# Moving the normalized rows' tiles to the weights' address modulo 512 bytes

## The chip, the cores and the metric

The kernel runs on one core of one Trainium2 chip. The metric is the device time of one execution in microseconds. Before the change it is 1011.47 us, the median of three runs that lie between 1011.24 and 1011.87 us.

## What is computed

Two layers of a decoder trunk on 256 rows of 1024 float32 values. Each layer has three sub-layers, and each of them normalizes the rows, scales and shifts them by a conditioning vector, and adds a gated result back:

```
h = modulate(rms_norm(x, norm_ffn1[l]), sh1, sc1)
x = x + 0.5 * g1 * swiglu(h, ffn1_w_in[l], ffn1_w_out[l])      # 1024 -> 2 x 2816 -> 1024
h = modulate(rms_norm(x, norm_mix[l]), sh2, sc2)
x = x + g2 * token_mix(h, ..., mix_w_in[l], ..., mix_w_out[l])  # gMLP half and sparse attention half
h = modulate(rms_norm(x, norm_ffn2[l]), sh3, sc3)
x = x + 0.5 * g3 * swiglu(h, ffn2_w_in[l], ffn2_w_out[l])
...
return rms_norm(x, final_norm)
```

The nine vectors `sh`, `sc`, `g` of a layer are `silu(c) @ ada_w[l] + ada_b[l]`.

## The kernel before, in words

**Precision.** Every float32 product of rows and weights is made of three products in the type float32r: high part by high part, and the two mixed ones. A weight tile `raw` (128 partitions x 4096 bytes) comes in by a DMA, ScalarE writes its high part `whi` (L474), VectorE the rest `wlo` (L479). There are 7 raw buffers and 10 of each part. The rows after normalization and modulation lie transposed in `hThi` and `hTlo`, 8192 bytes a partition each: two batches of 128 rows, eight blocks of 128 features, 512 bytes a block. The gated activations of the feed-forward lie in `aThi` and `aTlo` in blocks of 512 bytes, too.

**Six phases, three kinds of matmul.** The phases are feed-forward, mixing, feed-forward in layer 0, and the same in layer 1.

- In a feed-forward's input projection (`joint_chunk`, L694) the weights are the stationary operand, in 128-column slices, and the rows move: 256 columns, made of 128 columns of each batch 4096 bytes apart. Each matmul has a weight load of its own. There are 3648 of them: 1056 in the first feed-forward and 864 in each of the others, 24 for a weight tile.
- In the other input projections (the first 512 columns of feed-forwards 2 to 4 in `ffn_gen`, the mixing's in `mix_gen`) and in the mixing's output projection the rows `hThi`, `hTlo` are stationary, and the weights move, 512 columns at a time (L515 to L517, helper `mm3`): 960 matmuls, 288 of them in `ffn_gen`, and 96 with 324 columns.
- In a feed-forward's output projection (`project`) `aThi`, `aTlo` are stationary and the weights move by the same three lines: 990 matmuls of 512 columns. In the last phase the second batch's second half is cut in two, and there 132 of these matmuls have 256 columns.

**Order.** The schedule is written out by hand: each engine works in the order of the program. Between weight tiles the conditioning weights `ada_w` are streamed through the same raw buffers, and VectorE sums them up in `aacc` (L459). SyncE issues nearly all DMAs.

**Addresses.** The pool `const` hands out its tiles one behind the other in the order of the code. In the built program `hThi` begins at byte 36544 of each partition and `hTlo` at 44736: both are 192 modulo 512. `x` and `xm` are 64 modulo 512, `ident` 128, `ones` 192. The tiles `raw`, `whi`, `wlo`, `aacc`, `vec`, `aThi`, `aTlo` lie in other pools behind it, and all begin at 0 modulo 512.

The lines of the matmuls in question:

```
T.matmul(o, wk[stat][col], mov[:, :, k, :], start=..., stop=False, ...)   # L694
T.matmul(ps, ahi, whi, start=first, stop=False)                            # L515
T.matmul(ps, ahi, wlo, start=False, stop=False)                            # L516
T.matmul(ps, alo, whi, start=False, stop=last)                             # L517
```

In each the first operand behind the output is the stationary one. In the names of a row, `bank<-hThi,whi`, the moving one stands first.

Of the kernel before, what the change touches and what calls it, by code (L numbers as in the profile page):

```python
# [9 lines left out]
F32 = mybir.dt.float32  # L10
# [6 lines left out]
P = 128  # L17
D = 1024
KD = D // P
DFF = 2816  # L20
KF = DFF // P
DEPTH = 2
# [77 lines left out]
def trunk(ctx, tc, x_in, c_in, pos_in, ada_w, ada_b, norm_ffn1, ffn1_w_in, ffn1_w_out,  # L100
# [3 lines left out]
    V, S, G, T = nc.vector, nc.scalar, nc.gpsimd, nc.tensor  # L104
    ctx.enter_context(tc.manual_schedule())
    const = ctx.enter_context(tc.tile_pool(name="const", bufs=1))
# [25 lines left out]
    V.memset(negm, 1.0)  # L132
    ones = const.tile([P, P], F32R, name="ones")
    V.tensor_copy(ones, negm[:, :P])
    mhalf = const.tile([P, 16], F32, name="mhalf")[:, :1]
    G.memset(mhalf, -0.5)

    def causal_mask():
        G.memset(negm, 0.0)
# [61 lines left out]

    x = [const.tile([P, D], F32, name=f"x{b}") for b in range(2)]
    xm = [const.tile([P, D], F32, name=f"xm{b}") for b in range(2)]
    cols = const.tile([P, DEPTH, 96], F32, name="cols")
    ab = const.tile([P, DEPTH, 3, 2, KD], F32, name="ab")
    accs = [None]
    hThi = const.tile([P, 2, KD, P], F32R, name="hThi")
    hTlo = const.tile([P, 2, KD, P], F32R, name="hTlo")
    ang = const.tile([P, 2, 8], F32, name="ang")
    hT = [(hThi[:, b], hTlo[:, b]) for b in range(2)]  # L210

# [1122 lines left out]
```

## Time and profile before

| | |
|---|---|
| median of the runs | 1011.47 us |
| the profiled execution's own time | 1015.82 us |
| its span | 1014.1 us |
| TensorE (PE) busy | 986.3 us, 97% |
| weight loads (PEld) busy | 881.0 us, 87% |
| VectorE (DVE) busy | 777.9 us, 77% |
| ScalarE (ACT) busy | 536.3 us, 53% |
| bytes moved by DMA | 253.41 MB, 250 GB/s |

The span is what the profile's rows cover; the profiled execution took 1.7 us more than that, and 4.35 us more than the median. Times in the rows count from the span's start. The busy time of PE counts matmuls by ends that are modelled and that overlap. How fast a dense stream of matmuls runs is therefore read from the distance between their starts, or from how many lie in a window, and not from the duration of one.

### The profile page before, as it was taken

The numbers are of one execution on the slowest core, as the hardware profiler recorded it, in microseconds if no ns is written. First come the engines' busy times: TensorE is split into PE (matmuls) and PEld (weight loads), VectorE is DVE, ScalarE is ACT, GpSimd is POOL, SyncE is SP. The second block draws the span as 40 slices with busy tenths as digits, with TensorE's granted clock in tenths as the row PEclk, the third lists the DMA queues.
The fourth block names the chain that finished last, engine by engine and source line by source line (L and its number), as shares of the span: only waits on it lengthen the run. The fifth ranks groups of instructions, "written<-read, shape, count | busy, mean of one in ns | idle before, by whom it ended". The sixth has DMA issues, their size and how long they took to land.

```text
span 1014.1 us, 16715 instructions
## 1 busy us (share of the span) xinstructions
PE 986.3 (97%) x6468; PEld 881.0 (87%) x6468; DVE 777.9 (77%) x1088; ACT 536.3 (53%) x804; POOL 26.4 (3%) x39
## 2 busy tenths in 40 slices
PE   7999997999999999999999999999999999999997
PEld 6899995887787899998888999878778889999886
DVE  6888988777897877789678688895878785576554
ACT  6465454356577744545455454543657765454341
POOL 4000000000000000000000000000000000000000
PEclk9999998999999999999999999989999999999999
DMA  9988899956655577889858779987554556576731
GB/s 333 380 286 321 316 352 353 356 181 225 188 189 157 169 270 280 300 314 356 289 162 315 276 291 344 358 328 235 167 152 138 166 158 207 169 252 243 262 115 42
DMA packets 110031, 253.41 MB, mean 250 GB/s; under 512 B 8754, under 2 KB 27236, under 8 KB 109952
## 3 DMA queue, kind: packets, MB, share of 16 engines
q1 hardware_dynamic: 109120, 251.20, 70.8%
q8 instruction: 50, 0.82, 0.3%
q0 software_dynamic: 544, 0.63, 0.3%
q10 hardware_dynamic: 288, 0.52, 0.1%
q14 instruction: 29, 0.24, 0.1%
HBM read 251.27 MB, written 1.05 MB: 249 GB/s over the span
## 4 chain that ended last, share of the span: by engine, by line
PE 73%; DVE 12%; DMA 7%; ACT 5%; issue 3%; POOL 0%; SPq 0%; POOLq 0%; ACTq 0%; DVEq 0%
PE bank L694 28%; PE bank L515 14%; PE bank L517 13%; PE bank L516 13%; DVE wlo L479 3%; DVE aacc L459 3%; PE bank L780 2%; DMA raw<-in_ffn_w_in_dram 2%; DMA raw<-in_ffn_w_out_dram 2%; DMA sraw<-in_ada_w_dram 2%; ACT whi L474 2%; DVE xm L717 1%; ACT aThi L511 1%; DMA raw<-in_ada_w_dram 1%; DVE aacc L1101 1%
## 5 line engine op out<-in xcount | busy, mean ns | idle before, releaser
L474 ACT ACTIVATE whi<-raw 128x1024 fp32r<-128x1024 f32 (+1 forms) x328 | 334.9, 1046 | 233.1 <-PE bank L517 126.6
L479 DVE TENSOR_TENSOR wlo<-raw,whi 128x1024 fp32r<-128x1024 f32 (+1 forms) x313 | 373.9, 1212 | 91.7 <-ACT whi L474 89.7
L694 PE MATMUL bank<-hThi,whi 128*128 128x256 f32 x1216 | 336.1, 280 | 1.6 <-ACT hThi L1139 1.6
L694 PE MATMUL bank<-hThi,wlo 128*128 128x256 f32 x1216 | 333.2, 277 | 0.0
L694 PE MATMUL bank<-hTlo,whi 128*128 128x256 f32 x1216 | 323.7, 277 | 0.0
L694 PEld LDWEIGHTS bank<-hThi,whi 128*128 128x128 f32 x1216 | 228.3, 188 | 2.9 <-ACT hThi L1139 2.0
L694 PEld LDWEIGHTS bank<-hThi,wlo 128*128 128x128 f32 x1216 | 229.1, 188 | 0.7 <-issue 0.7
L694 PEld LDWEIGHTS bank<-hTlo,whi 128*128 128x128 f32 x1216 | 222.6, 188 | 0.3
L515 PE MATMUL bank<-whi,aThi 128*128 128x512 f32 (+1 forms) x374 | 144.1, 385 | 1.4 <-ACT whi L474 1.3
L516 PE MATMUL bank<-wlo,aThi 128*128 128x512 f32 (+1 forms) x374 | 143.2, 383 | 2.3 <-DVE wlo L479 2.3
L459 DVE SCALAR_TENSOR_TENSOR aacc<-raw,ccol,aacc 128x1024 f32<-128x1024 f32 x112 | 143.5, 1281 | 1.2 <-DMA raw<-in_ada_w_dram 1.2
L517 PE MATMUL bank<-whi,aTlo 128*128 128x512 f32 (+1 forms) x374 | 142.7, 381 | 0.0
L515 PE MATMUL bank<-whi,hThi 128*128 128x512 f32 (+1 forms) x352 | 140.9, 400 | 0.7 <-ACT hThi L560 0.7
L517 PE MATMUL bank<-whi,hTlo 128*128 128x512 f32 (+1 forms) x352 | 136.2, 387 | 0.0
L516 PE MATMUL bank<-wlo,hThi 128*128 128x512 f32 (+1 forms) x352 | 135.1, 384 | 0.0
L516 PEld LDWEIGHTS bank<-wlo,aThi 128*128 128x128 f32 x374 | 71.4, 191 | 16.1 <-DVE wlo L479 3.3
L515 PEld LDWEIGHTS bank<-whi,aThi 128*128 128x128 f32 x374 | 71.5, 191 | 15.3 <-ACT whi L474 1.8
L517 PEld LDWEIGHTS bank<-whi,aTlo 128*128 128x128 f32 x374 | 71.3, 191 | 13.5
L515 PEld LDWEIGHTS bank<-whi,hThi 128*128 128x128 f32 x352 | 66.2, 188 | 16.9 <-issue 2.0
L517 PEld LDWEIGHTS bank<-whi,hTlo 128*128 128x128 f32 x352 | 66.1, 188 | 14.9 <-DVE hTlo L561 0.9
L516 PEld LDWEIGHTS bank<-wlo,hThi 128*128 128x128 f32 x352 | 66.3, 188 | 11.6
L717 DVE TENSOR_TENSOR xm<-xm,bank 128x256 f32<-128x256 f32 x76 | 29.5, 416 | 54.5 <-ACT xm L716 54.4
(158 smaller groups left out, 692.5 us busy)
## 6 DMA issues: line engine op xcount, KB each, us to landing
raw<-in_ffn_w_in_dram SPq DMA_DIRECT2D x160, 512.0 KB, 5.7
raw<-in_ada_w_dram SPq DMA_DIRECT2D x128, 512.0 KB, 5.8
raw<-in_ffn_w_out_dram SPq DMA_DIRECT2D x88, 512.0 KB, 6.3
raw<-in_mix_w_in_dram SPq DMA_DIRECT2D x40, 512.0 KB, 4.4
sraw<-in_ada_w_dram SPq DMA_DIRECT2D x32, 256.0 KB, 6.1
raw<-in_ffn_w_in_dram SPq DMA_DIRECT2D x32, 256.0 KB, 3.5
raw<-in_mix_w_out_dram SPq DMA_DIRECT2D x16, 512.0 KB, 3.7
vec<-in_ada_b_dram SPq DMA_DIRECT2D x6, 512.0 KB, 7.5
```

The lines of the kernel that those rows point to most:

```text
L459: V.scalar_tensor_tensor(aacc, e["raw"], ccol[:, j:j + 1], aacc, op0=ALU.mult, op1=ALU.add)
L474: S.activation(hi[:, :n], src, AF.Copy)
L479: V.tensor_tensor(lo[:, :n], src, hi[:, :n].bitcast(F32), op=ALU.subtract)
L511: S.activation(hi, ps, AF.Copy)
L515: T.matmul(ps, ahi, whi, start=first, stop=False)
L516: T.matmul(ps, ahi, wlo, start=False, stop=False)
L517: T.matmul(ps, alo, whi, start=False, stop=last)
L694: T.matmul(o, wk[stat][col], mov[:, :, k, :], start=first and i_ == 0 and mov is hThi and stat == 0, stop=False, skip_group_check=True)
L717: V.tensor_tensor(a, a, acc[j][:, 256:], op=ALU.mult)
L780: T.transpose(ps[:, i * P:(i + 1) * P], src(i), ident)
L1101: V.scalar_tensor_tensor(acc, su[g][j], ccol[:, j:j + 1], su["dps"] if j == PEJ else acc, op0=ALU.mult, op1=ALU.add)
```

## The change

Three constants are allocated elsewhere. `mhalf` (64 bytes, a constant for the reciprocal root) stood ahead of everything from `posi` on, `cols` (768 bytes) and `ab` (384 bytes) stood ahead of `hThi`. All three now stand behind `hTlo`. In the built program after the change `x` and `xm` begin at 0 modulo 512, and so do `hThi` (byte 35328) and `hTlo` (43520). From `ang` on, every tile lies where it lay.

```
-    mhalf = const.tile([P, 16], F32, name="mhalf")[:, :1]
-    G.memset(mhalf, -0.5)
...
-    cols = const.tile([P, DEPTH, 96], F32, name="cols")
-    ab = const.tile([P, DEPTH, 3, 2, KD], F32, name="ab")
     accs = [None]
     hThi = const.tile([P, 2, KD, P], F32R, name="hThi")
     hTlo = const.tile([P, 2, KD, P], F32R, name="hTlo")
+    cols = const.tile([P, DEPTH, 96], F32, name="cols")
+    ab = const.tile([P, DEPTH, 3, 2, KD], F32, name="ab")
+    mhalf = const.tile([P, 16], F32, name="mhalf")[:, :1]
+    G.memset(mhalf, -0.5)
```

No instruction is added or taken away, and none changes its place on its engine; line numbers and buffer numbers are all that differs. The one statement that moves in the code is the memset of `mhalf` on GpSimd. This is the beginning of that engine's work, before (-) and after (+):

```order
 masks.py:199 ISA
 masks.py:199 AFFINE_SELECT ident<-ident 128x128
-L136 MEMSET mhalf 128x1
+L208 MEMSET mhalf 128x1
 L1154 DMA rows<-in_ada_b_dram 72x128
 L1156 DMA rows<-in_norm_ffn_dram 8x128
```

It stands behind the identity matrix and ahead of the first load both times: only its line number moved.

## Rows read from the trace of the kernel before

**Rows 1.** The page, part 4: the chain that ended last, by line.
```profile
PE bank L694 28%; PE bank L515 14%; PE bank L517 13%; PE bank L516 13%; DVE wlo L479 3%; DVE aacc L459 3%; PE bank L780 2%; DMA raw<-in_ffn_w_in_dram 2%; DMA raw<-in_ffn_w_out_dram 2%; DMA sraw<-in_ada_w_dram 2%; ACT whi L474 2%; DVE xm L717 1%; ACT aThi L511 1%; DMA raw<-in_ada_w_dram 1%; DVE aacc L1101 1%
```

**Rows 2.** Groups by line and shape: count | busy, mean ns of one | idle before.
```profile
L694 PE MATMUL bank<-hThi,whi 128*128 128x256 f32 x1216 | 336.1, 280 | 1.6 <-ACT hThi L1139 1.6
...
L511 ACT ACTIVATE aThi<-xm 128x512 fp32r<-128x512 f32 x38 | 24.0, 635 | 35.9 <-DVE xm L717 35.9
...
L560 ACT ACTIVATE hThi<-xm 128x512 fp32r<-128x512 f32 x20 | 11.5, 624 | 0.3
```

**Rows 3.** L694 alone in five windows: length, PE, weight loads, clock, DMA, GB/s.
```profile
53.30:91.30 38.00, 37.85 (x320) 37.59 (x319) 1.00 0.85 302
138.80:152.40 13.60, 13.60 (x118) 13.60 (x117) 1.00 0.98 355
404.60:444.00 39.40, 39.40 (x336) 39.38 (x335) 1.00 0.79 297
586.90:592.50 5.60, 5.60 (x48) 5.43 (x47) 1.00 0.96 312
856.00:945.00 89.00, 89.00 (x786) 88.81 (x784) 1.00 0.62 222
```

**Rows 4.** PE's instructions in order of time around 404 us: start, duration.
```profile
403.42 0.28 PE L694 MATMUL bank<-hThi,wlo 128*128 128x256 f32 x1
...
404.44 0.28 PE L694 MATMUL bank<-hThi,whi 128*128 128x256 f32 x1
404.56 0.28 PE L694 MATMUL bank<-hTlo,whi 128*128 128x256 f32 x1
```

**Rows 5.** The same at the end of the last output projection, all operands aligned.
```profile
1004.64 0.28 PE L515 MATMUL bank<-whi,aThi 128*128 128x256 f32 x1
1004.76 0.28 PE L516 MATMUL bank<-wlo,aThi 128*128 128x256 f32 x1
1004.88 0.28 PE L517 MATMUL bank<-whi,aTlo 128*128 128x256 f32 x1
...
1006.08 0.28 PE L515 MATMUL bank<-whi,aThi 128*128 128x256 f32 x1
```

**Rows 6.** The same in mixing's output projection, `hThi`, `hTlo` stationary: first and tenth.
```profile
824.25 0.39 PE L517 MATMUL bank<-whi,hTlo 128*128 128x512 f32 x1
...
826.32 0.39 PE L517 MATMUL bank<-whi,hTlo 128*128 128x512 f32 x1
```

**Rows 7.** The same in an output projection, `aThi`, `aTlo` stationary: first and tenth.
```profile
679.30 0.39 PE L517 MATMUL bank<-whi,aTlo 128*128 128x512 f32 x1
...
681.34 0.39 PE L517 MATMUL bank<-whi,aTlo 128*128 128x512 f32 x1
```

**Rows 8.** PE behind the first input projection: what it waited for, in brackets.
```profile
172.17 0.79 PE L374 MATMUL bank<-whi,ones 128*128 128x512 f32 x1 [5.93 <-ACT whi L474]
173.43 0.79 PE L375 MATMUL bank<-wlo,ones 128*128 128x512 f32 x1 [0.47 <-DVE wlo L479]
```

**Rows 9.** PE behind layer 1's first input projection, likewise.
```profile
658.93 0.50 PE L515 MATMUL bank<-whi,aThi 128*128 128x512 f32 x1 [1.35 <-ACT whi L474]
661.04 0.79 PE L516 MATMUL bank<-wlo,aThi 128*128 128x512 f32 x1 [1.61 <-DVE wlo L479]
```

**Rows 10.** ACT in these two projections: where it last waited long for PE.
```profile
80.58 0.38 ACT L716 ACTIVATE xm<-bank 128x256 f32<-128x256 f32 x1 [2.98 <-PE bank L694]
...
624.80 0.38 ACT L716 ACTIVATE xm<-bank 128x256 f32<-128x256 f32 x1 [3.13 <-PE bank L694]
```

**Rows 11.** All engines in two windows behind these projections; PEclk is the granted clock.
```profile
170.00:180.00 10.00, 7.36 (x19) 5.50 (x20) 8.78 (x11) 5.35 (x6) 0.00 (x0) 0.57 0.75 256
660.00:670.00 10.00, 8.96 (x32) 7.24 (x33) 9.71 (x9) 4.05 (x5) 0.00 (x0) 0.66 0.79 278
```

**Rows 12.** PE in the first of them, two matmuls at the lower clock.
```profile
176.15 0.63 PE L515 MATMUL bank<-whi,aThi 128*128 128x512 f32 x1
176.58 0.63 PE L516 MATMUL bank<-wlo,aThi 128*128 128x512 f32 x1
```

## The prediction, made before the run

> **What bounds the kernel now.** I read the chain of waits first. The weight matmuls stand at its head: L694 has 28% of the span, L515 to L517 together 40% [rows 1]. TensorE is the bound over most of the program, so the question is how fast a dense stream of matmuls runs. The durations in the groups don't tell that, since they overlap: a 256-column matmul of L694 is listed with 280 ns [rows 2], but 786 of them lie in 89 us. So I counted matmuls in windows. A window also counts what is under way at its edges, about two; I take two off each. In layer 1's last input projection the pace is 89.0 / 784 = 113.5 ns a matmul. Between 404.6 and 444.0 us the same instruction at the same full clock takes 39.4 / 334 = 118.0 ns [rows 3]. Nothing waits in either stretch. So L694 has two paces, and each lasts for hundreds of matmuls. The first row of the group, with 318 in 38 us and one short break in it, is a third long stretch at the slow pace, and 138.8 to 152.4 us a fourth (13.6 / 116 = 117 ns). Of the short ones of some 46 there are two, and one stands. Together 318 + 116 + 334 + 2 x 46 = 860 of the 3648 are slow, nearly all others fast. What flips the pace can be seen at 404 us: four matmuls of another line come in between, and from the first start behind them, 404.44 us, the distance is 0.12 us, where it had been 0.11 before [rows 4]. So what matters is how a weight load and the running matmul meet in time, and that is where an address can enter.
>
> **What the change does.** It moves no instruction. It moves where `hThi` and `hTlo` begin, from 192 to 0 modulo 512 bytes, where all weights begin; `x` and `xm` go from 64 to 0. For ScalarE and VectorE I cost this at nothing: the same copy takes 624 ns into `hThi`, which is off by 192, and 635 ns into `aThi`, which isn't [rows 2]. The memset of `mhalf` stays at its place on GpSimd. What is left are two kinds of matmul, and for both the trace of before has a stretch in which all operands are aligned already, since `aThi` and the weights are.
>
> *Rows stationary, 512 columns (960 matmuls).* With `hTlo` and `hThi` stationary nine steps take 826.32 - 824.25 = 2.07 us, or 230 ns each [rows 6]; with `aThi` and `aTlo`, the same helper and the same moving weights, nine take 681.34 - 679.30 = 2.04 us, or 226.7 ns [rows 7]. The reading is to 0.01 us, so the gain is 3.3 ns give or take 1. At 3.3 ns the 288 of `ffn_gen` bring 0.95 us and the 672 of the two mixings 2.2 us; but a mixing also waits for its attention, so not all of the second counts. Bounds: 0.7 us (the first at 2.3 ns alone) to 3.2 us. I take **-1.5 us**.
>
> *Rows moving, 256 columns (3648 matmuls).* The nearest row is the very end of the last output projection, where 256 columns move and everything is at 0 modulo 512. There twelve steps from 1004.64 to 1006.08 us take 1.44 us: **120 ns**, from the first to the last [rows 5]. That isn't the fast pace, and it is slower than the slow one. The stream comes into it from 512-column matmuls and stays at 120 for as long as the 256-column ones last, while with 192 bytes between the operands the fast pace lasts for 784 matmuls. Two things differ from L694: the 256 columns are in one piece, not in two 4096 bytes apart, and the part that is stationary there moves here. Modulo 512 the moving addresses are the same sequence. I take 120 ns for all of L694. The bounds are 113.5 ns for all of it and 120 ns for all of it.
>
> The sum by stage, with 6.5 ns for each fast matmul and 2.0 ns for each slow one:
> - start, up to 53 us: 224 x 6.5 = 1.5 us. PE waits there for the conditioning that DMA and VectorE bring; I keep 0.3.
> - layer 0, first feed-forward: 832 matmuls, 434 of them slow: 398 x 6.5 + 434 x 2.0 = 3.5 us.
> - layer 0, second: 334 slow: 530 x 6.5 + 334 x 2.0 = 4.1 us.
> - layer 1, first: 92 slow: 772 x 6.5 + 92 x 2.0 = 5.2 us.
> - layer 1, second: 864 x 6.5 = 5.6 us.
>
> All together 19.9 us. Part of it is hidden, since PE waits behind two of these stages: 5.93 + 0.47 us at 172 us for weights that DMA, ScalarE and VectorE haven't made ready [rows 8], and 1.35 + 1.61 us at 659 us [rows 9]. ScalarE last waited long for PE at 80.58 us in the first and at 624.80 us in the other [rows 10]. From there on the supply runs by itself, and a slower PE only arrives later at a wait that ends when it ended before. In the first stage that hides all but the part before 81 us, (81 - 53) / 0.118 = 235 x 2.0 = 0.5 us kept. In the other the last 24.4 us are hidden, 215 x 6.5 = 1.4 us, and 3.8 are kept. Behind the other two stages nothing waits, and all is kept. So 0.3 + 0.5 + 4.1 + 3.8 + 5.6 = **+14.3 us**.
>
> One thing may go either way: behind both waits the granted clock falls (means of 0.57 and 0.66 in the windows [rows 11]), and matmuls of 512 columns start 0.43 us apart instead of 0.227 [rows 12]: that is the lower level, 1.2 GHz instead of 2.4. By these means 0.43 x 2 x 10 = 8.6 us of the first window and 6.8 us of the other lie at the lower level; less PE's idle time in them, 2.6 and 1.0 us, some 6 us of work are left in each, 14 steps that cost 0.2 us more, 2.8 us. What the engine did before the clock fell was to wait. Shorter waits may spare one or both of them (-5.6 us at most), or only shift the fall so that more work lies in it (+1.4 for each, by the time that the wait gets shorter). I take nothing.
>
> The sum is 14.3 - 1.5 = **+12.8 us**: 1028.6 us against the profiled execution's own 1015.8, and 1024.3 against the median of 1011.47, which is what I forecast.
>
> A rule of the Trainium skill speaks against any effect. "TensorE: Matmul & The Clock Gate" (Step-by-step: what each phase is for) says that loading the next tile's weights takes no read bandwidth from the running matmul, since the two have ports of their own; "SBUF — State Buffer" (Who interferes with whom) says that TensorE never waits for another engine's accesses. By this rule addresses would not matter and the change would bring 0. The two paces of L694 and the 3.3 ns between the two kinds of stationary tile don't agree with it.
>
> **The rivals.**
> - *Aligned is the fast pace.* For it: at 512 columns the aligned stream is the faster one [rows 6, 7], and the end of the last projection may be slow because of how it is entered, from 512 columns. Against it: there it stays slow for twelve steps and more. Then the 860 slow matmuls gain 4.5 ns each, 3.9 us; 203 of them lie in the supply-bound part of the first stage (91.3 - 81 us, and 138.8 to 152.4), so 0.9 of it becomes a wait, and 3.0 stays. With the 1.5 us of the other kind: 1007.0 us.
> - *L694 stays as it is.* Two paces by accident of entry, not of address; only the stationary kind gains: 1010.0 us.
> - *Addresses change nothing at all*, and the 3.3 ns come from what other engines do in the mixing. Beside this stands the rule quoted above. Then 1011.5 us.
>
> That the change wouldn't do what it says is ruled out by the addresses of the built program. The forecast is the one slower case among these, and the first rival ends on the other side by the same instruction. Between them decides L694's mean pace. Today it is (2788 x 113.5 + 860 x 118) / 3648 = 114.6 ns; the 1.5 us of the other kind pay for 0.4 ns more, so above some 115 ns the change loses, if nothing is hidden.
>
> **How the numbers follow.** Aligned L694 at 120 ns: 0.62; its own range is 1018 (both falls of the clock gone) to 1032 us (nothing hidden, 19.9 - 0.7 us, and the falls dearer). Aligned is fast: 0.18. L694 unchanged: 0.12. No effect: 0.08. To leave out no more than two in ten the range has to reach the fast case, so 1006.5 to 1032. A measurement of this kernel can tell 0.2% from no change, about 2 us, so 1010.0 and 1011.5 both count as the same. Faster: 0.18 and a little of the next case, 0.20. Same: 0.18. Slower: 0.62.
>
> **What the profile after would show.** In the windows of L694 a pace of 120 ns everywhere, 742 matmuls in 89 us instead of 784, and weight loads a little longer; where 113.5 ns stand everywhere, the first rival is right. In the mixing's output projection nine steps should take 2.04 us. The waits of 5.93 and 1.35 + 1.61 us should be shorter by some 3 and 1.4 us; if they are not, the supply does wait for PE, and my term for what is hidden is wrong. If L694 shows the two paces as before in about the same shares, the address modulo 512 isn't what decides.

## The result, and the profile after

The changed kernel takes 1024.49 us (median of 4 runs, 1023.57 to 1026.7), the kernel before 1011.67 us in its 4 runs (1011.24 to 1012.74). The ratio is 1.0128, with a 95% interval of 1.011 to 1.0147: 12.8 us slower, as forecast to 0.2 us. The profiled execution took 1024.0 us, its span was 1022.2 us.

TensorE's weight matmuls still head the chain, and L694 has grown in it from 28% to 33%, which answers [rows 1]. The page of the kernel after, part 4:

```profile
PE bank L694 33%; PE bank L515 13%; PE bank L517 13%; PE bank L516 13%; DVE wlo L479 3%; DMA raw<-in_ffn_w_in_dram 3%; PE bank L780 2%; DVE aacc L459 2%; ACT whi L474 1%; DMA raw<-in_ffn_w_out_dram 1%; DMA raw<-in_ada_w_dram 1%; DMA sraw<-in_ada_w_dram 1%; DVE xm L717 1%; ACT xm L553 1%; ACT aThi L511 1%
```

L694 alone in windows of its dense stretches (kernel after; window, length, PE busy and count, weight loads busy and count, granted clock, DMA share, GB/s), against [rows 3]:

```profile
60.00:91.00 31.00, 31.00 (x260) 31.00 (x259) 1.00 0.88 313
406.00:446.00 40.00, 39.83 (x332) 39.96 (x333) 1.00 0.76 288
858.50:950.00 91.50, 91.50 (x765) 91.50 (x764) 1.00 0.57 207
```

Taking two off each count as before, the paces are 31.0 / 258 = 120.2, 39.83 / 330 = 120.7 and 91.5 / 763 = 119.9 ns. Scaled to the forecast's 89 us, the last is 742 matmuls. There is one pace now, everywhere, and it is the 120 ns that stood at the end of the last output projection [rows 5]. The granted clock is 1.00 in all three windows, as it was before: the same matmul at the same clock takes longer. Over all pairs of L694 matmuls that start one behind the other without a break (3598 of them) the distance from start to start is 119.95 ns on the mean, against 114.46 ns in the trace before.

The listed durations show a little of it. Groups by line and shape of the kernel after (count, then busy us, mean ns of one, idle before); the first answers a line of [rows 2], and the weight load was 222.6 us, 188 ns each before:

```profile
L694 PE MATMUL bank<-hThi,whi 128*128 128x256 f32 x1216 | 343.5, 285 | 1.6 <-ACT hThi L1139 1.6
...
L694 PEld LDWEIGHTS bank<-hTlo,whi 128*128 128x128 f32 x1216 | 227.4, 192 | 0.2
```

In the mixing's output projection, with `hTlo` and `hThi` stationary, the first and the tenth of a run of steps (timeline of PE, start and duration) answer [rows 6]:

```profile
824.19 0.39 PE L517 MATMUL bank<-whi,hTlo 128*128 128x512 f32 x1
...
826.23 0.39 PE L517 MATMUL bank<-whi,hTlo 128*128 128x512 f32 x1
```

Nine steps take 2.04 us, as with `aThi` in [rows 7]. What PE waits for behind the two first input projections (timeline, the wait in brackets) answers [rows 8, 9]:

```profile
172.83 0.79 PE L374 MATMUL bank<-whi,ones 128*128 128x512 f32 x1 [5.92 <-ACT whi L474]
...
666.59 0.50 PE L516 MATMUL bank<-wlo,aThi 128*128 128x512 f32 x1 [0.38 <-DVE wlo L479]
```

And the two windows of [rows 11], all engines, granted clock third from the end:

```profile
170.00:180.00 10.00, 6.70 (x21) 5.06 (x22) 8.78 (x11) 5.76 (x6) 0.00 (x0) 0.66 0.75 239
660.00:670.00 10.00, 9.62 (x45) 7.67 (x44) 8.60 (x14) 6.65 (x9) 0.00 (x0) 1.00 0.81 304
```

The long wait at 172 us stands as it was. The waits behind layer 1's projection went from 1.35 + 1.61 to 0.38 us, and the clock no longer falls behind them.

### The profile page after: what moved, and what is told of

Same layout as the page of the kernel before. It is cut to its first block, busy times and chain, and to the rows that moved or that the text cites. A ratio compares the mean times of both kernels' runs of the same rounds, so it can differ in the third digit from the quotient of the medians.

```text
span 1022.2 us, 16715 instructions
## 1 busy us (share of the span) xinstructions
PE 1000.8 (98%) x6468; PEld 899.0 (88%) x6468; DVE 778.3 (76%) x1088; ACT 536.3 (52%) x804; POOL 26.4 (3%) x39
## 4 chain that ended last, share of the span: by engine, by line
PE 77%; DVE 9%; DMA 6%; ACT 4%; issue 2%; SPq 0%; POOL 0%; POOLq 0%; ACTq 0%; DVEq 0%
PE bank L694 33%; PE bank L515 13%; PE bank L517 13%; PE bank L516 13%; DVE wlo L479 3%; DMA raw<-in_ffn_w_in_dram 3%; PE bank L780 2%; DVE aacc L459 2%; ACT whi L474 1%; DMA raw<-in_ffn_w_out_dram 1%; DMA raw<-in_ada_w_dram 1%; DMA sraw<-in_ada_w_dram 1%; DVE xm L717 1%; ACT xm L553 1%; ACT aThi L511 1%
## 5 line engine op out<-in xcount | busy, mean ns | idle before, releaser
L474 ACT ACTIVATE whi<-raw 128x1024 fp32r<-128x1024 f32 (+1 forms) x328 | 334.8, 1046 | 230.7 <-PE bank L517 113.2
L694 PE MATMUL bank<-hThi,whi 128*128 128x256 f32 x1216 | 343.5, 285 | 1.6 <-ACT hThi L1139 1.6
L694 PE MATMUL bank<-hThi,wlo 128*128 128x256 f32 x1216 | 340.7, 283 | 0.0
L694 PE MATMUL bank<-hTlo,whi 128*128 128x256 f32 x1216 | 330.6, 283 | 0.0
L694 PEld LDWEIGHTS bank<-hThi,whi 128*128 128x128 f32 x1216 | 233.4, 192 | 2.9 <-ACT hThi L1139 2.0
L694 PEld LDWEIGHTS bank<-hThi,wlo 128*128 128x128 f32 x1216 | 233.4, 192 | 0.7 <-DVE hTlo L1141 0.5
L694 PEld LDWEIGHTS bank<-hTlo,whi 128*128 128x128 f32 x1216 | 227.4, 192 | 0.2
L717 DVE TENSOR_TENSOR xm<-xm,bank 128x256 f32<-128x256 f32 x76 | 29.6, 417 | 68.1 <-ACT xm L716 68.1
```

The lines of the kernel that those rows point to most:

```text
L474: S.activation(hi[:, :n], src, AF.Copy)
L694: T.matmul(o, wk[stat][col], mov[:, :, k, :], start=first and i_ == 0 and mov is hThi and stat == 0, stop=False, skip_group_check=True)
L717: V.tensor_tensor(a, a, acc[j][:, 256:], op=ALU.mult)
```

## The experiments

The question behind all of them: does the distance between the start of the moving tile and that of the weights, modulo 512 bytes, set the pace, or is it something else that the change did? Every kernel but the one profiled once more is the one after with a few unused tiles of padding, and computes the whole reference. "Distance" is the start of `hThi` and `hTlo` less the start of the weights. The kernel before has 192, the one after 0. Line numbers shift by two to four with the padding: L694 reads L696 to L698.

### The weights moved in place of the rows

```
     rawp = ctx.enter_context(tc.tile_pool(name="rawp", bufs=NRAW))
+    padp = ctx.enter_context(tc.tile_pool(name="padp", bufs=1))
+    pad0 = padp.tile([P, 80], F32, name="pad0")
     hlp = ctx.enter_context(tc.tile_pool(name="hlp", bufs=NB))
+    padq = ctx.enter_context(tc.tile_pool(name="padq", bufs=1))
+    pad1 = padq.tile([P, 48], F32, name="pad1")
```

The weights lie at 320 and the rows at 0, which makes the distance 192 modulo 512 again.

> Changed kernel, but the ten whi and ten wlo buffers begin at 320 modulo 512 (a pad of 320 bytes ahead of them, 192 behind), with hThi and hTlo at 0: the distance between rows and weights is 192 again, as in the kernel before, with other tiles than there moved. Theory (the distance modulo 512 between the moving and the stationary tile sets L694's pace): L694 leaves 120 ns and has the paces of before, 113.5 ns for most matmuls and 118 for the rest, and the output projections, where aThi stays at 0 and the weights now don't, go from 226.7 to about 230 ns a step (990 matmuls, +3 us): some 1014 to 1016 us. Rival (the rows' own address is what counts, or any tile at 0): L694 stays at 120 ns, 1025 us or more.

Measured: 1013.18 us (10 runs, 1011.54 to 1015.53), ratio 1.0014 [1.0002, 1.0025], a little below the 1014 to 1016 expected. The profiled execution is the slowest of the ten. L694 alone in two windows (columns as above):

```profile
406.00:436.00 30.00, 30.00 (x267) 30.00 (x266) 1.00 0.87 325
...
860.00:900.00 40.00, 40.00 (x342) 40.00 (x342) 1.00 0.62 223
```

30.0 / 265 = 113.2 ns and 40.0 / 340 = 117.6 ns: both old paces are back with the rows still at 0, so it isn't the rows' own address that counts. `aThi` and `aTlo`, which lie at 0 and stand still here, now have the distance 192 too. Over some 920 of their steps the mean from start to start is 229.5 ns, where it is 227.9 in the trace before; nine of them take 2.06 us where [rows 7] has 2.04 (timeline, first and tenth):

```profile
679.77 0.39 PE L521 MATMUL bank<-whi,aTlo 128*128 128x512 f32 x1
...
681.83 0.39 PE L521 MATMUL bank<-whi,aTlo 128*128 128x512 f32 x1
```

Both kinds follow the distance to the weights. These two stretches have swapped their paces, though: in the trace before, 406 to 436 us is at the slow one and the last stage at the fast one. In all, 1941 of 3596 starts of this profile lie more than 115 ns behind the one ahead, against 913 before, so "113.5 ns for most" wasn't met.

### `x` and `xm` back where they were

```
+    pad0 = const.tile([P, 16], F32, name="pad0")
     x = [const.tile([P, D], F32, name=f"x{b}") for b in range(2)]
     xm = [const.tile([P, D], F32, name=f"xm{b}") for b in range(2)]
     accs = [None]
+    pad1 = const.tile([P, 112], F32, name="pad1")
     hThi = const.tile([P, 2, KD, P], F32R, name="hThi")
```

`x` and `xm` at 64 as before, the rows at 0 as after.

> Changed kernel with x and xm back at 64 modulo 512 (a pad ahead of x) and hThi, hTlo at 0. Theory (only the rows' tiles matter): as the changed kernel, 1024.5 us, L694 at 120 ns throughout. Rival (x and xm, or the transposes that read them, have a part): between 1011.5 and 1024.5 us.

Measured: 1024.42 us, ratio 1.0129 [1.0112, 1.0146], the same as after. L694 in the last stage:

```profile
870.00:940.00 70.00, 70.00 (x586) 70.00 (x585) 1.00 0.56 198
```

70.0 / 584 = 119.9 ns. With the rows at 0, the place of `xm` does nothing: the loss comes with `hThi` and `hTlo`.

### The rows alone back where they were

```
     accs = [None]
+    pad0 = const.tile([P, 48], F32, name="pad0")
     hThi = const.tile([P, 2, KD, P], F32R, name="hThi")
     hTlo = const.tile([P, 2, KD, P], F32R, name="hTlo")
+    pad1 = const.tile([P, 80], F32, name="pad1")
```

The rows at 192, `x` and `xm` at 0.

> Changed kernel with a pad that puts hThi and hTlo back to 192 modulo 512; x and xm stay at 0, and cols, ab and mhalf stay behind hTlo. Theory: as the kernel before, 1011.5 us within 0.2%, L694 in its two paces of 113.5 and 118 ns. Rival (the three constants or x and xm have a part): over 1014 us.

Measured: 1016.12 us (1015.34 to 1018.25), ratio 1.0047 [1.003, 1.0064]. That is a miss: two thirds of the loss come back, and 4.4 us stay. L694 alone in three windows:

```profile
372.00:400.00 28.00, 28.00 (x240) 28.00 (x240) 1.00 0.62 218
...
406.00:436.00 30.00, 30.00 (x267) 30.00 (x267) 1.00 0.84 314
...
860.00:900.00 40.00, 40.00 (x342) 40.00 (x342) 1.00 0.62 223
```

28.0 / 238 = 117.6, 30.0 / 265 = 113.2, 40.0 / 340 = 117.6 ns. The two paces are back, but the first and the third of these stretches run at the slow one, where the kernel before runs them fast, and the second is the other way round. In all 2035 of 3595 starts are at the slow pace (more than 115 ns behind the one ahead), against 913 in the first trace of the kernel before. So there is a second thing that picks the pace. The last run below looks for it.

### The kernel before, profiled once more

> The kernel before once more, for a second profile. In the first profile TensorE waited 1.35 and 1.61 us at 659 us and its clock fell behind that; that execution took 4.35 us more than the median. Theory (that wait and fall belong to this one execution, since the median lies 4 us lower): the second profile has shorter waits there, no fall at 660 us, and a span of some 1009 to 1010 us. Rival (they belong to the kernel): the same waits and the same fall again, span 1014 us.

Measured: 1011.82 us with a span of 1010.0 us, where the first profile had 1015.82 and 1014.1. Behind layer 1's first projection one wait is left, and the clock doesn't fall (timeline, and all engines in a window):

```profile
659.63 0.50 PE L516 MATMUL bank<-wlo,aThi 128*128 128x512 f32 x1 [1.57 <-DVE wlo L479]
```

```profile
660.00:670.00 10.00, 10.00 (x49) 8.23 (x48) 10.00 (x10) 4.13 (x5) 0.00 (x0) 1.00 0.94 349
```

The granted clock is 1.00 where [rows 11] has 0.66, in the same kernel. So the fall of the clock at 660 us belonged to the one execution that the prediction read, and its absence after is not the change's doing. The output projection there takes 68.9 us in the first profile and 64.6 in this one. The mix of paces varies as well: 1092 starts at the slow pace here, 913 there, the difference being in the main one stretch of 192 matmuls at 110.9 us (117.8 ns here, 113.5 there). The comparison by stage below uses this profile, whose time is the median's.

### A sweep of the distance

Seven kernels differ from the one after by two tiles, `pad0` ahead of `hThi` and `pad1` behind `hTlo`, 512 bytes together; `x` and `xm` stay at 0. The one for 64 bytes:

```
+    pad0 = const.tile([P, 16], F32, name="pad0")
     hThi = const.tile([P, 2, KD, P], F32R, name="hThi")
     hTlo = const.tile([P, 2, KD, P], F32R, name="hTlo")
+    pad1 = const.tile([P, 112], F32, name="pad1")
```

64 bytes:

> Rows' tiles hThi, hTlo at 64 modulo 512, all else as in the changed kernel. Theory (the distance modulo 512 sets how weight load and running matmul meet, and 0 is one bad distance among others): L694 has a pace of its own here, anywhere from 113.5 to 120 ns; near to 0, so I expect it nearer to 120 than to 113.5, and 1016 to 1025 us. Rival (0 alone is bad, every other distance is like 192): the paces of 113.5 and 118 ns, 1011 to 1016 us.

128 bytes:

> Rows' tiles at 128 modulo 512. Theory: between 64 and 192, L694 at 113.5 to 118 ns, 1010 to 1018 us. Rival (0 alone is bad): the two paces of the kernel before, 1011 to 1016 us.

256 bytes:

> Rows' tiles at 256 modulo 512, the farthest from 0. Theory: if distance is what helps, the fast pace of 113.5 ns for nearly all of L694 and 1007 to 1009 us. Rival (the period is 256 bytes or less and not 512): as at 0, 120 ns and 1024 us.

320 bytes:

> Rows' tiles at 320 modulo 512, which is 192 below the weights. Theory (what counts is the distance, with its sign): a pace of its own, 113.5 to 118 ns, 1007 to 1016 us. Rival (the sign doesn't count): the two paces of 192, 1011 to 1016 us.

448 bytes:

> Rows' tiles at 448 modulo 512. At 0 and 256 L694 ran at 120 ns, at 64 and 320 at 117.4. Theory (the period is 256 bytes): 448 is as 192, with the two paces of 113.5 and 118 ns, and a time between 1008 and 1016 us that depends on which pace each stage falls into. Rival (the period is 512, and 0 and 256 are alike by chance): a pace of its own, such as 117 to 120 ns throughout, over 1018 us.

160 bytes:

> Rows' tiles at 160 modulo 512, a multiple of 32 but not of 64 bytes. Theory (only the distance modulo 256 counts): a pace between those at 128 (118.7 ns) and at 192 (113.5 and 118 ns), 1008 to 1024 us. Rival (a start that isn't a multiple of 64 bytes costs by itself): over 120 ns, and over 1026 us.

224 bytes:

> Rows' tiles at 224 modulo 512. Theory: a pace between those at 192 (113.5 and 118 ns) and at 256 (120 ns), 1008 to 1024 us; if the fast pace is the only one here, 1007 to 1009 us, and it would beat the kernel before. Rival (a start that isn't a multiple of 64 bytes costs by itself): over 120 ns, and over 1026 us.

L694 alone in the same stretch of the last stage, kernel by kernel. 64 bytes:

```profile
870.00:940.00 70.00, 70.00 (x597) 70.00 (x596) 1.00 0.57 204
```

128 bytes:

```profile
870.00:940.00 70.00, 70.00 (x592) 70.00 (x591) 1.00 0.57 205
```

160 bytes:

```profile
870.00:940.00 70.00, 70.00 (x599) 70.00 (x598) 1.00 0.58 207
```

224 bytes:

```profile
870.00:940.00 70.00, 70.00 (x593) 70.00 (x593) 1.00 0.57 203
```

256 bytes:

```profile
870.00:940.00 70.00, 70.00 (x586) 70.00 (x585) 1.00 0.57 199
```

320 bytes:

```profile
870.00:940.00 70.00, 70.00 (x597) 70.00 (x596) 1.00 0.58 205
```

448 bytes, with a stretch at the other pace:

```profile
406.00:436.00 30.00, 30.00 (x267) 30.00 (x266) 1.00 0.86 316
...
860.00:900.00 40.00, 40.00 (x342) 40.00 (x342) 1.00 0.62 224
```

These windows lie in one stretch each, and a kernel can hold more than one pace. L694 at 64 bytes, in an earlier stretch:

```profile
61.00:89.00 28.00, 28.00 (x250) 28.00 (x249) 1.00 0.90 317
```

128 bytes, likewise:

```profile
360.00:367.00 7.00, 7.00 (x60) 7.00 (x60) 1.00 0.99 360
```

160 bytes, likewise:

```profile
408.00:447.00 39.00, 39.00 (x330) 39.00 (x330) 1.00 0.78 293
```

Less two, they are 28.0 / 248 = 112.9, 7.0 / 58 = 120.7 and 39.0 / 328 = 118.9 ns. By the starts themselves, stretch by stretch, the paces are 113.3 ns over 262 starts, 119.9 over 71 and 118.7 over 335.

The same by the distance, with the mean from start to start of 512-column matmuls that have `hThi` or `hTlo` stationary (837 of them that follow without a break), and the times:

| distance | L694, ns | 512 columns, ns | median us | ratio [95%] |
|---|---|---|---|---|
| 0 (after) | 119.9 | 228.2 | 1024.49 | 1.0128 [1.011, 1.0147] |
| 64 | 70 / 595 = 117.6, one stretch 113.3 | 233.3 | 1022.57 | 1.0105 [1.0044, 1.0167] |
| 128 | 70 / 590 = 118.6, three stretches of 71 at 120 | 232.3 | 1024.73 | 1.0127 [1.0068, 1.0185] |
| 160 | 70 / 597 = 117.3, or 118.7 | 233.5 | 1023.24 | 1.0114 [1.0084, 1.0144] |
| 192 (rows alone back) | 113.2 or 117.6 | 229.4 | 1016.12 | 1.0047 [1.003, 1.0064] |
| 224 | 70 / 591 = 118.4 | 233.3 | 1024.53 | 1.0127 [1.0098, 1.0156] |
| 256 | 70 / 584 = 119.9 | 228.2 | 1024.51 | 1.0124 [1.0066, 1.0182] |
| 320 | 70 / 595 = 117.6, one long stretch 113.3 | 233.4 | 1023.12 | 1.0111 [1.0055, 1.0166] |
| 448 | 113.2 or 117.6 | 229.4 | 1016.51 | 1.0048 [1.0025, 1.0071] |

256 gives what 0 gives, 320 what 64 gives, 448 what 192 gives, in both columns. In these three pairs the pattern repeats after 256 bytes, so the change's "modulo 512" is finer than it need be. Two paces in one kernel aren't special to 192 and 448: 64 and 320 have the same two, but there only 263 and 285 of some 3600 starts are at the fast one (no more than 115 ns behind the one ahead), against 1560 and 1548 in the kernels with the rows at 192 and 448 and `xm` at 0. A mean over the whole program hides this (117.45 ns at 64). So the distance sets which paces there are, and something else which of them a stretch takes. At 0, 224 and 256 one pace holds for all stretches. The stationary kind orders the distances otherwise: it is quickest where L694 is slowest.

Several expectations missed. At 128 (1010 to 1018 us expected), 256 (1007 to 1009) and 320 (1007 to 1016) the kernels take 1023 to 1025 us, and at 224 and 448 the time lies half a us above the range. What was called the rival at 256, a period of 256 bytes or less, is what the runs show. At 64 the time is the theory's, but the paces are the rival's two.

### `xm` back beside the rows

```
     x = [const.tile([P, D], F32, name=f"x{b}") for b in range(2)]
+    pad0 = const.tile([P, 16], F32, name="pad0")
     xm = [const.tile([P, D], F32, name=f"xm{b}") for b in range(2)]
     accs = [None]
+    pad1 = const.tile([P, 32], F32, name="pad1")
     hThi = const.tile([P, 2, KD, P], F32R, name="hThi")
     hTlo = const.tile([P, 2, KD, P], F32R, name="hTlo")
+    pad2 = const.tile([P, 80], F32, name="pad2")
```

`xm` at 64 and the rows at 192 as before, `x` at 0 as after. Of the three kernels with the rows at 192, this one and the kernel before have `xm` at 64.

> As the kernel with the rows' tiles back at 192 and x, xm at 0 (1016.1 us, where every long stretch of L694 behind a transpose of xm is slow, the last of them with 790 matmuls), but xm at 64 again as in the kernel before; x stays at 0. Theory (a transpose of xm loads xm as the stationary operand, and its address sets in which of the two paces the stream behind it starts): the stretches behind transposes of xm are fast again, as in the kernel before, the one with 790 matmuls among them; 1011.5 to 1012.5 us. Rival (x or the three constants behind hTlo did it): those stretches stay slow, 1016 us.

Measured: 1011.11 us (10 runs, 1008.22 to 1013.26), ratio 1.0004 [0.9995, 1.0014]: the time of before. L694 in the three windows of the kernel with the rows alone back:

```profile
372.00:400.00 28.00, 28.00 (x249) 28.00 (x249) 1.00 0.76 265
...
406.00:436.00 30.00, 30.00 (x257) 30.00 (x256) 1.00 0.85 321
...
860.00:900.00 40.00, 40.00 (x355) 40.00 (x354) 1.00 0.56 195
```

28.0 / 247 = 113.4, 30.0 / 255 = 117.6 and 40.0 / 353 = 113.3 ns: fast, slow, fast, as in the kernel before, and the reverse of what it was with `xm` at 0. `xm` isn't an operand of L694. It is the stationary operand of the transposes (L780 before) that come in between, and no other operand of TensorE was moved between the two kernels. ScalarE and VectorE write and read `xm`, too; their two largest groups on it take the same in both (378 and 417 ns on the mean), but that `xm` acts through the transposes isn't shown by itself. The timelines at the entry to the last stage; with `xm` at 64:

```profile
847.09 0.60 PE L783 MATMUL bank<-ident,xm 128*128 128x128 f32 x4
847.44 0.37 PE L697 MATMUL bank<-hThi,whi 128*128 128x256 f32 x1
847.65 0.28 PE L697 MATMUL bank<-hTlo,whi 128*128 128x256 f32 x1
```

and with `xm` at 0, in the kernel with the rows alone back:

```profile
853.61 0.60 PE L782 MATMUL bank<-ident,xm 128*128 128x128 f32 x4
853.97 0.37 PE L696 MATMUL bank<-hThi,whi 128*128 128x256 f32 x1
854.17 0.28 PE L696 MATMUL bank<-hTlo,whi 128*128 128x256 f32 x1
```

0.35 us from the transposes to the stream in the one, 0.36 in the other, which is no more than the reading's last digit. The traces keep starts in whole ns, and there the entries do differ: from the last matmul ahead to the first transpose 122 ns in the one and 115 in the other, from the first matmul of the stream to the second 207 and 203. What follows from the one is 790 starts at 113.3 ns, from the other 790 at 117.8.

One execution could have fallen so by chance, as a stretch did in the two profiles of before. But from layer 0's second input projection on all three profiles with `xm` at 64 (two of before, one of this kernel) have the same pace in each of the 14 stretches, and so have the two with `xm` at 0 (rows at 192 and at 448) among themselves. The two patterns differ in five of the 14, the longest included: 1336 starts are slow in these five with `xm` at 0 and 335 with it at 64, and 1001 x 4.5 ns = 4.5 us is about the time between the kernels.

## Why the prediction was right, step by step

The lengths of the stages, from the first matmul of one to the first of the next (us; "in" is the input projection with L694, "out" its output projection):

| stage | before, first profile | before, second | after | after less second | predicted |
|---|---|---|---|---|---|
| start, up to layer 0's first feed-forward | 17.7 | 17.9 | 17.4 | -0.5 | +0.3 (up to 53 us) |
| layer 0, first, in + out | 135.0 + 74.9 | 136.2 + 73.7 | 137.1 + 72.6 | -0.2 | +0.5 |
| layer 0, second, in + out | 101.7 + 62.7 | 101.7 + 62.7 | 105.9 + 62.7 | +4.2 | +4.1 |
| layer 1, first, in + out | 102.0 + 68.9 | 102.0 + 64.6 | 107.2 + 63.4 | +4.0 | +3.8 |
| layer 1, second, in + out | 98.4 + 61.8 | 98.4 + 61.8 | 104.1 + 61.8 | +5.7 | +5.6 |
| mixings and the 512 columns between | 283.6 | 283.6 | 282.7 | -0.9 | -1.5 |
| all of these | 1006.7 | 1002.6 | 1014.9 | +12.3 | +12.8 |

That the total is met to half a us here, and to 0.2 us in the medians, is in part luck: the first two lines of the table together came out 1.5 us lower than their terms, the mixings 0.6 us higher.

**The pace of L694** was read from twelve steps of another line at the very end of the program, and held: 119.95 ns over 3598 starts against the 120 forecast. By the means of the starts, 119.95 - 114.69 = 5.26 ns, 3648 matmuls lose 19.2 us against the second profile, and 20.0 against the first, where the working had 19.9. The two input projections with nothing behind them to hide in, and the one that is hidden in part, came out within 0.2 us each. The row that the pace was read from has the parts of the two operands exchanged; the prediction gave it a chance of 0.62, and it held.

From the rule of the Trainium skill that was weighed there ("TensorE: Matmul & The Clock Gate", Step-by-step: what each phase is for, and "SBUF — State Buffer", Who interferes with whom), which is about ports and other engines, the prediction had concluded that addresses wouldn't matter. By the runs the start of a tile costs or spares 12 us of this kernel, so that conclusion doesn't hold here.

**What is hidden** had the right size and, in layer 0, the wrong place. From its first matmul to the end of its output projection, layer 0's first feed-forward takes 209.9, 209.9 and 209.7 us in the three profiles, although L694's mean pace in it is 115.3, 116.1 and 119.9 ns: a slower PE is hidden there, as the prediction said. But it wanted the wait at 172 us shorter by some 3 us, and that wait is 5.93 us before and 5.92 after. The step that failed is that the slower PE would only arrive later at this wait. Both ends of the wait hang on VectorE. PE's last six matmuls ahead of it begin when L717 on VectorE is done, and the chain that leads from there to the high part it then waits for runs over ScalarE and VectorE alone. The weight load of the first of the six and the end of the wait, in the second profile of before:

```profile
165.47 0.19 PEld L515 LDWEIGHTS bank<-whi,aThi 128*128 128x128 f32 x1 [0.53 <-DVE xm L717]
...
173.07 0.80 PE L374 MATMUL bank<-whi,ones 128*128 128x512 f32 x1 [5.94 <-ACT whi L474]
```

The same weight load in the first profile of before, where the wait ends at 172.17 us [rows 8]:

```profile
164.57 0.19 PEld L515 LDWEIGHTS bank<-whi,aThi 128*128 128x128 f32 x1 [0.52 <-DVE xm L717]
```

and after, where it ends at 172.83 us:

```profile
165.24 0.19 PEld L515 LDWEIGHTS bank<-whi,aThi 128*128 128x128 f32 x1 [0.42 <-DVE xm L717]
```

From the one to the other it is 7.60, 7.60 and 7.59 us, wherever it lies. Nor does its end follow PE's pace: it is later in the second profile of before, at 116.1 ns, than after, at 119.9. And the supply doesn't run quite by itself from 81 us on. In the second profile of before ScalarE waits for L694 once more:

```profile
130.89 1.06 ACT L474 ACTIVATE whi<-raw 128x1024 fp32r<-128x1024 f32 x1 [1.44 <-PE bank L694]
```

What took up the slower pace were smaller waits, most of them inside the projection. PE alone from 18 to 156 us (length, PE busy and count, clock, DMA share, GB/s), the kernel before in its second profile:

```profile
18.00:156.00 138.00, 134.88 (x1106) 1.00 0.92 331
```

and the kernel after:

```profile
18.00:156.00 138.00, 137.49 (x1102) 1.00 0.93 333
```

PE is idle there for 3.12 us before and 0.51 us after. The largest piece, in the second profile of before, is gone after:

```profile
109.88 0.50 PE L374 MATMUL bank<-whi,ones 128*128 128x512 f32 x1 [1.94 <-DVE xm L717]
```

So I took the wait with the largest number for the one that would give way. In layer 1 the place was right: 1.57 us of waiting (1.35 + 1.61 in the first profile) became 0.38, 1.2 us hidden against 1.4 foreseen.

**The stationary kind** gained less: -0.9 us for -1.5. Over all dense starts it went from 229.4 to 228.2 ns, 1.25 ns and not 3.3; 960 x 1.25 = 1.2 us, not 3.2. The nine steps of [rows 6] and [rows 7] were a fair reading of those 2 us but a poor sample: the means over the program are 229.4 for `hThi` and 227.9 for `aThi`. The bounds had 0.7 at the low end, so the range held it.

**The clock** was taken as nothing. The fall at 172 us stays (0.57 and 0.66 in the windows of the first profile and after, and 0.66 in the second profile of before, too). The one at 660 us is gone, but so it is in the second profile of before, so nothing was gained by the change. It is why the profile pair that the prediction reasoned on gives only 1022.2 - 1014.1 = +8.1 us, while medians and the second pair of spans give +12.8 and +12.2.

**The rivals.** Aligned is not the fast pace: no L694 stretch after has it. L694 unchanged and no effect at all are out by the same rows. Of "two paces by accident of entry" one half is true all the same. With 192 bytes between the operands the entry does choose, and the address of `xm` changes how; with 0 bytes there is nothing to choose from.

**What stays open.** Why TensorE has these paces at these distances isn't shown; no row tells what the weight load and the moving rows meet in, and that they meet in time is the prediction's reading. Nor is the rule of the choice shown: with `xm` at 0 and the rows at 192 or 448 there is one pattern, with `xm` at 64 another, and with the weights at 320 in place of the rows a third, read from one execution whose time was not the median's. That the choice hangs on a few nanoseconds at the entry has more for it than the two timelines above. In the five profiles with the rows at 192 or 448, of the stretches of 40 and more that follow transposes all 22 slow ones begin with a first step of 202 or 203 ns, and 46 of the 48 fast ones with 200, 201 or 205 to 208. The first step may be the choice's effect as well as its cause. No kernel here beat the one before; the best of them had its time.

## What to carry to other kernels

Where a dense stream of matmuls bounds a kernel, count their starts in a window without waits, stretch by stretch: listed durations overlap and hardly move (280 to 285 ns here, for 5% of pace). If one instruction at one clock has two paces, look at where its moving tile and its weights begin, and compare with a stretch of the trace in which these lie otherwise; a new small constant in the same pool can move them. "Aligned" is no goal of itself: here the distance of 0 was, with 256, the slowest of all that were tried for rows that move, and the best for rows that stand still.

## What the runs showed of the hardware

- The start of the moving tile against that of the weights sets which paces 256-column float32r matmuls have at the full clock: 119.9 ns at 0 and 256 bytes, 118.6 at 128 (120 in three short stretches), 118.4 at 224, 117.3 or 118.7 at 160, and 113.3 or 117.8 at 64, 192, 320 and 448. The three pairs that lie 256 bytes apart agree, so the period is 256 bytes and not the 512 of the change.
- Where there are two paces, each is kept for up to 790 matmuls until something else runs in between. At 64 and 320 bytes nearly all stretches take the slow one. At 192 a tile that isn't an operand of this stream, `xm`, changed which stretches take it, moved by 64 bytes: 762 starts at the slow pace with `xm` at 64, 2035 with it at 0, and 1011.1 against 1016.1 us.
- With 512 columns moving the order of the distances is another: 228.2 ns at 0 and 256, 229.4 at 192 and 448, 232.3 at 128, and 233.3 to 233.5 at 64, 160, 224 and 320.
- Two executions of the same kernel can differ by a stretch at the other pace and by a fall of the clock (1014.1 and 1010.0 us of span), which is as much as some changes are worth. One profile of before was not enough to read a difference by stage.
